# One list for projections, decode and attention, with pages two at a time

## The chip, the cores and the metric

The kernel runs on one core of a Trainium2 chip. The metric is device time in microseconds (us) of one execution; lower is better. Before the change the median of three runs is 1311.23 us (1310.11 to 1312.16).

## What is computed

One inference step of a two-layer trunk on 512 prompt tokens and on 8 x 4 sample tokens (32 rows), which are handled together as 544 columns. Layer 0 mixes tokens by a convolution module, layer 1 by stick-breaking attention with 16 heads of 64; each is followed by a ConvFFN (1024 to 2816 and back). The change touches layer 1's mixer alone, and the planner that orders several stages:

```python
qkv = (h @ attn_w_qkv[a]).reshape(b, t, 3, N_HEADS, HEAD_DIM)
q, k, v = qkv[:, :, 0], qkv[:, :, 1], qkv[:, :, 2]
k_all = jnp.concatenate([k_past[a], k], axis=1)
...
z = jnp.einsum('bqhd,bkhd->bhqk', q, k) * (HEAD_DIM ** -0.5) + bias
log_fail = jnp.where(valid, jax.nn.log_sigmoid(-z), 0.0)
after = lax.cumsum(log_fail, axis=3, reverse=True) - log_fail
weights = jnp.where(valid, jnp.exp(jax.nn.log_sigmoid(z) + after), 0.0)
out = jnp.einsum('bhqk,bkhd->bqhd', weights, v)
```

The prompt has no past. Each of the 8 sample sequences has 256 past positions, in two pages of 128 rows of a paged pool of keys and one of values. The new key and value rows are outputs too.

## The kernel before

Activations lie transposed: chunk c of 8 holds 128 channels (two heads) on the partitions and 544 tokens in the free dimension, in two streams, `SA` (256 columns) and `SB` (288, the sample tokens among them). Each projection is taken in three passes of rounded parts: weights and inputs are split into high and low (`whi`, `wlo`; `XH`, `XL`), and high x high, high x low and low x high are added. A chunk's weights are one slot (`W`, five slots at a time); ScalarE makes `whi` (L342), VectorE `wlo` (L345) from a 1 MB `raw` tile that SP's queue loads. A slot is 24 matmuls for `SA` and 24 for `SB`.

In program order around the change:

1. Queries of all chunks. `xT`, the residual, is stored to DRAM (`xsave`), and its place takes pages of the cache (`page_t`, three of them), decode weights (`wT`) and scratch.
2. The key stage, written out by hand. The keys of eight chunks are projected (`gemm`, L432 to L434); between the matmuls stand hooks. `page_turn` transposes a page of keys in eight 128x128 transposes (L1921), which VectorE and ScalarE copy out of PSUM half by half (L1922); `page_logits` multiplies it with `Qz`, eight products with 32 columns of weights each (L1934), of which four stand side by side in the array. An f32 product is two instructions. Rows of the new keys go back by transposes (L1883, and L1885 for the 32 sample rows).
3. The attention stage, a `Plan`: operations with an engine, an estimated cost and what they read and write; `Plan.run` (L162) emits them by simulated time, choosing for each engine the least of start time minus a share of the rank (the longest chain behind it), and its order is the engines' program order. PSUM tiles of one tag are handed out in the order of the list, and each waits for the users of the one before it in its bank. `values` projects value chunks (L2073 to L2075), `decode_weights` the sample tokens' weights, `page` multiplies one page of values with them (L2160, 32 columns of weights), `new_values` adds the new tokens' part (L2182), `pair` is a pair of heads on the prompt: in three units (`UNITS`) logits (L2214, 64 rows, two heads side by side in the array and in two banks of `z`), exponentials, suffix sums on VectorE, transposes (L2254, tag `t`), and products with the values (L2263, 64 columns of weights, two heads side by side, one trip for each unit). The pair's output goes through `qT` into `XH` and `XL` (L2292, L2293). Behind them `xT` returns from DRAM (L2288), and four chunks of the output projection begin in the attention stage's banks.
4. The rest of the output projection (L432 to L434 again), and from the adds of L2320 on the second ConvFFN.

The same `Plan.run` orders the convolution stage at the start and both ConvFFNs.

Of the kernel before, what the change touches and what calls it, by code (L numbers as in the profile page):

```python
# [73 lines left out]
STICK = 0.2  # L74
HI, LO = 0.59, 1.23

BIG = 1.0e17
E_BUFS, S_BUFS, W_BUFS = 3, 2, 3


class Plan:
# [15 lines left out]
    def op(self, eng, cost, fn, r=(), w=(), a=(), follows=None, lift=0.0, urgent=0.0, after=()):  # L97
# [33 lines left out]
        if follows is not None:  # L131
            self.follows[i] = follows
        return i
# [28 lines left out]
    def run(self):  # L162
# [16 lines left out]
        free, last = {}, {}  # L179
        while any(ready.values()):  # L180
            best = None
            for eng, q in ready.items():
                if q:
                    f = free.get(eng, 0.0)
                    i = min(q, key=lambda i: (max(f, start[i]) - self.eager * rank[i] - self.urgent.get(i, 0.0) -
                                              (STICK if self.follows.get(i, -1) == last.get(eng) else 0.0), i))
# [6 lines left out]
            fn()  # L193
            last[eng] = i
# [9 lines left out]
def tile_trunk(  # L204
# [78 lines left out]
    for c in range(0, 3 * NC, 2):  # L283
        both(attn_w_qkv[0], 0, NC, c)
    for c in range(0, NC, 2):
        both(attn_w_o[0], 0, NC, c)
# [1552 lines left out]
    pages = deque()  # L1839
    n_page = [0]  # L1840

    def gather():

        i = n_page[0]
        if i >= 4 * NB:
            return
        n_page[0] += 1
        t = page_t[i % PAGE_BUFS]
        j = i % (2 * NB)
        pool.indirect_dma_start(out=t, out_offset=None, in_=ck if i < 2 * NB else cv,  # L1850
                                in_offset=bass.IndirectOffsetOnAxis(ap=idx[:, j:j + 1], axis=0))
        pages.append(t)


    for _ in range(PAGE_BUFS):
        gather()

    q_all.stream(SB, hooked=False)
    d1_cm, d1 = open_pool("d1")
    Qz = d1.tile([P, NC, 2, 160], F32, name="Qz")  # L1860
    Qf = d1.tile([P, NC, 2, NS], F32, name="Qf")
    pool.memset(Qz, 0.0)
    pool.memset(Qf, 0.0)
    for bg in range(2):
        for j in range(2):
            rows = slice(j * HD, (j + 1) * HD)
            src = qT[rows, :, SEQ + 16 * bg:SEQ + 16 * bg + 16].rearrange("p c (b i) -> p c b i", b=4)
            dst = Qz[rows, :, bg, :].rearrange("p c (b s) -> p c b s", s=40)[:, :, :, 4 * j:4 * j + 4]
            pool.tensor_copy(dst, src)
            dst = Qf[rows, :, bg, :].rearrange("p c (b s) -> p c b s", s=8)[:, :, :, 4 * j:4 * j + 4]  # L1870
            pool.tensor_copy(dst, src)
# [3 lines left out]
    ps_cm, ps = open_pool("ps_qkv", space=PSUM)  # L1875
    banks.update(acc=3, tr=2, one=1)

    def rows_of(src, n, dst, dst_s):


        def turn(pt):
            for b in range(2):
                pe.transpose(pt[:, b * P:(b + 1) * P], src[:, b * P:(b + 1) * P], ident)  # L1883
            if n > 256:
                pe.transpose(pt[:NS, 256:256 + P], src[:, 256:n], ident)  # L1885

        def store(pt):
            dve.tensor_copy(dst, pt[:, :256].rearrange("p (b d) -> p b d", b=2))

        def store_s(pt):  # L1890
            if n > 256:
                act.copy(dst_s, pt[:NS, 256:256 + P])

        def steps():
            pt = bank("tr", uid("rows"))
            for f in (turn, store, store_s):
                f(pt)

        steps.parts = turn, store, store_s
        return steps  # L1900

# [4 lines left out]

# [458 lines left out]
```

## Time and profile before

| | us |
|---|---|
| median of 3 runs | 1311.23 (1310.11 to 1312.16) |
| span of the profiled execution | 1311.1 |
| TensorE busy (matmul / weight load) | 1292.6 / 1224.0 |
| VectorE, ScalarE, GpSimd busy | 985.8, 720.8, 158.8 |
| key stage, attention stage | 653 to 735, 735 to 884 |

The profile is that of one execution; its span is the time from the first to the last instruction. Busy times of TensorE overlap since matmuls are pipelined; where its time goes is better read from the starts of its instructions. "Idle before" names what ended an engine's wait.

### The profile page before, as it was taken

The numbers are of one execution on the slowest core, as the hardware profiler recorded it, in microseconds if no ns is written. First come the engines' busy times: TensorE is split into PE (matmuls) and PEld (weight loads), VectorE is DVE, ScalarE is ACT, GpSimd is POOL, SyncE is SP. The second block draws the span as 40 slices with busy tenths as digits, with TensorE's granted clock in tenths as the row PEclk, the third lists the DMA queues.
The fourth block names the chain that finished last, engine by engine and source line by source line (L and its number), as shares of the span: only waits on it lengthen the run. The fifth ranks groups of instructions, "written<-read, shape, count | busy, mean of one in ns | idle before, by whom it ended". The sixth has DMA issues, their size and how long they took to land. (4 is left out here: it accounts for less than half of the span.)

```text
span 1311.1 us, 27036 instructions
## 1 busy us (share of the span) xinstructions
PE 1292.6 (99%) x11072; PEld 1224.0 (93%) x11072; DVE 985.8 (75%) x1679; ACT 720.8 (55%) x1440; POOL 158.8 (12%) x302
## 2 busy tenths in 40 slices
PE   8999999999999999999999999999999999999997
PEld 7998689999999999999999877789999999999997
DVE  6799885978987877868234688775997996886864
ACT  6477584545554544445323688863655564454453
POOL 4000013101010010000222113210010010010000
PEclk9999999999999999999999999999999999999999
DMA  7463523123232233234456224432223332223221
GB/s 205 122 183 100 155 66 113 33 82 113 89 113 91 78 105 111 73 123 166 145 177 188 91 86 135 128 129 65 81 66 113 97 114 90 89 89 108 89 75 69
DMA packets 116592, 142.43 MB, mean 109 GB/s; under 512 B 5364, under 2 KB 107528, under 8 KB 116195
## 3 DMA queue, kind: packets, MB, share of 16 engines
q1 hardware_dynamic: 107151, 111.89, 27.5%
q0 software_dynamic: 9024, 28.78, 7.0%
q8 instruction: 87, 1.43, 0.5%
q14 instruction: 38, 0.31, 0.1%
q10 hardware_dynamic: 292, 0.02, 0.0%
HBM read 129.34 MB, written 12.18 MB: 108 GB/s over the span
## 5 line engine op out<-in xcount | busy, mean ns | idle before, releaser
L342 ACT CAST whi<-raw 128x1024 fp32r<-128x1024 f32 (+2 forms) x245 | 223.3, 913 | 149.3 <-PE tr L1317 31.6
L345 DVE TENSOR_TENSOR wlo<-raw,whi 128x1024 fp32r<-128x1024 f32 (+2 forms) x245 | 256.5, 1051 | 57.1 <-ACT whi L342 56.0
L673 PE MATMUL acc<-XH,whi 128*128 128x288 f32 (+1 forms) x384 | 114.3, 298 | 0.0
L674 PE MATMUL acc<-XL,whi 128*128 128x288 f32 (+1 forms) x384 | 111.6, 290 | 0.0
L675 PE MATMUL acc<-XH,wlo 128*128 128x288 f32 (+1 forms) x384 | 111.1, 289 | 0.2 <-DVE wlo L345 0.2
L432 PE MATMUL acc<-XH,whi 128*128 128x288 f32 (+1 forms) x360 | 107.8, 299 | 1.6 <-DVE xT L2320 1.1
L434 PE MATMUL acc<-XH,wlo 128*128 128x288 f32 (+1 forms) x360 | 103.8, 288 | 0.5 <-DVE wlo L345 0.5
L433 PE MATMUL acc<-XL,whi 128*128 128x288 f32 (+1 forms) x360 | 103.9, 289 | 0.0
L1552 ACT COPY G<-acc 128x272 f32<-128x272 f32 (+1 forms) x72 | 26.9, 374 | 104.9 <-PE acc L1518 90.1
L1516 PE MATMUL acc<-TH,whi 128*128 128x272 f32 x288 | 82.9, 288 | 0.0
L1518 PE MATMUL acc<-TH,wlo 128*128 128x272 f32 x288 | 82.8, 288 | 0.0
L1517 PE MATMUL acc<-TL,whi 128*128 128x272 f32 x288 | 82.8, 287 | 0.0
L673 PEld LDWEIGHTS acc<-XH,whi 128*128 128x128 f32 x384 | 72.9, 190 | 3.0 <-issue 1.6
L1317 PE MATMUL av<-HL,whi 128*128 128x288 f32 (+1 forms) x256 | 74.6, 291 | 0.3 <-DVE HL L1570 0.3
L1316 PE MATMUL av<-HH,whi 128*128 128x288 f32 (+1 forms) x256 | 74.4, 291 | 0.0
L1318 PE MATMUL av<-HH,wlo 128*128 128x288 f32 (+1 forms) x256 | 74.0, 289 | 0.3 <-DVE wlo L345 0.3
L1316 PE MATMUL tr<-HH,whi 128*128 128x256 f32 (+1 forms) x256 | 73.4, 287 | 0.0
L674 PEld LDWEIGHTS acc<-XL,whi 128*128 128x128 f32 x384 | 73.0, 190 | 0.3
L1317 PE MATMUL tr<-HL,whi 128*128 128x256 f32 (+1 forms) x256 | 73.3, 286 | 0.0
L675 PEld LDWEIGHTS acc<-XH,wlo 128*128 128x128 f32 x384 | 72.9, 190 | 0.4 <-DVE wlo L345 0.4
L1318 PE MATMUL tr<-HH,wlo 128*128 128x256 f32 (+1 forms) x256 | 72.9, 285 | 0.0
L432 PEld LDWEIGHTS acc<-XH,whi 128*128 128x128 f32 x360 | 67.7, 188 | 4.6 <-issue 2.4
(402 smaller groups left out, 4349.1 us busy)
## 6 DMA issues: line engine op xcount, KB each, us to landing
raw<-in_ffn_w_gate_dram SPq DMA_DIRECT2D x22, 1024.0 KB
raw<-in_ffn_w_up_dram SPq DMA_DIRECT2D x22, 1024.0 KB
raw<-in_ffn_w_down_dram SPq DMA_DIRECT2D x24, 768.0 KB
raw<-in_attn_w_qkv_dram SPq DMA_DIRECT2D x12, 1024.0 KB
raw<-in_conv_w_in_dram POOLq DMA_DIRECT2D x6, 1024.0 KB
rep<-glu SPq DMA_DIRECT2D x36, 142.0 KB
raw<-in_conv_w_out_dram POOLq DMA_DIRECT2D x4, 1024.0 KB
raw<-in_ffn_w_down_dram SPq DMA_DIRECT2D x8, 512.0 KB
```

The lines of the kernel that those rows point to most:

```text
L342: act.copy(hi[:, k, :], src[:, k])
L345: dve.tensor_tensor(lo[:, k, :], src[:, k], hi[:, k, :], op=ALU.subtract)
L432: pe.matmul(o, hi[:, k, :], xh[:, k, c0:c0 + n], start=(k == 0), stop=False)
L433: pe.matmul(o, hi[:, k, :], xl[:, k, c0:c0 + n], start=False, stop=False)
L434: pe.matmul(o, lo[:, k, :], xh[:, k, c0:c0 + n], start=False, stop=(k == nk - 1))
L673: pe.matmul(o, hi[:, k, :], XH[:, k, c0:c0 + n], start=(k == 0), stop=False)
L674: pe.matmul(o, hi[:, k, :], XL[:, k, c0:c0 + n], start=False, stop=False)
L675: pe.matmul(o, lo[:, k, :], XH[:, k, c0:c0 + n], start=False, stop=(k == NC - 1))
L1316: pe.matmul(o, hi[:, j + k, :], xh, start=(start and k == 0), stop=False, **kw)
L1317: pe.matmul(o, hi[:, j + k, :], xl, start=False, stop=False, **kw)
L1318: pe.matmul(o, lo[:, j + k, :], xh, start=False, stop=(stop and k == len(xs) - 1), **kw)
L1516: pe.matmul(o, hi[:, j + k, :], xh, start=(start and k == 0), stop=False, **kw)
```

## The change

The key stage's loop goes, and its work joins the attention stage's `Plan`. Keys and values are projected in turn (`TURNS`: two key chunks, then a value chunk and a key chunk alternately), with their weights loaded in that order, and these projections are marked as `fill`. `page_logits` takes both pages of a sequence in one trip of 256 columns, with turned pages in the place of the last four chunks of `kT`; `sequence` multiplies both value pages in one trip; a pair's products go in one trip, save the last pair's. Sample columns of keys and values stay apart (`kT_s`, `vT_s`) and are turned all at once (`new_rows`); their weights form a block-diagonal matrix (`Zw`). The attention output's splits of the first seven pairs stand behind the last value projection, the last pair's are made from PSUM. PSUM's eight banks are dealt out anew. `Plan.run` gets a new key: work that starts within `NEAR` of the soonest goes ahead, in this list `fill` goes last, a change of shape (`form`) has a cost and waits up to `PATIENT`.

```diff
--- before.py
+++ after.py
...
+CHANGE, CHANGE_BIAS = 0.17, 3.0
...
-E_BUFS, S_BUFS, W_BUFS = 3, 2, 3
+E_BUFS, S_BUFS, W_BUFS = (3, 1), (1, 1), (3, 1)
+NEAR, PATIENT = 0.15, 2.0
...
-        free, last = {}, {}
+        free, last, form = {}, {}, None
...
+        def turned(i):
+            return self.change if self.change and self.ops[i][0] == "pe" and self.forms.get(i) != form else 0.0
...
-                    i = min(q, key=lambda i: (max(f, start[i]) - self.eager * rank[i] - self.urgent.get(i, 0.0) -
-                                              (STICK if self.follows.get(i, -1) == last.get(eng) else 0.0), i))
+                    soon = min(max(f, start[i]) for i in q) + NEAR
+
+                    def key(i):
+                        t, turn = max(f, start[i]), turned(i)
+                        later = t > soon or i in self.fill or (turn and self.fill and form is None and start[i] + PATIENT > soon)
+                        return (bool(later), t + CHANGE_BIAS * turn - self.eager * rank[i] - self.urgent.get(i, 0.0) -
+                                (STICK if self.follows.get(i, -1) == last.get(eng) else 0.0), i)
...
+            cost += turned(i)
+            if eng == "pe":
+                form = self.forms.get(i)
...
-    for c in range(0, 3 * NC, 2):
+    for c in range(0, NC, 2):
         both(attn_w_qkv[0], 0, NC, c)
+    TURNS = [("k", 0), ("k", 1)] + [x for c in range(NC) for x in (("v", c), ("k", c + 2)) if x[1] < NC]
...
+    specs.extend((r0 + c // 2 * 2 + (f == "v"), c % 2, c % 2 == 1, NC) for f, c in TURNS)
...
-    banks.update(acc=1, one=1, av=1, z=3, t=2)
+    banks.update(acc=2, one=1, dz=1, av=1, z=2, t=1)
...
-    def values(i, h):
...
+    def project(slot, h):
+
...
+        pt = psum("acc")
...
+            last = plan.op("pe", 6 * n * COL, weighted(pt, slot, h, q), w=[pt], follows=last, after=[] if last is None else [last],
+                           r=[("slot", slot), ("X", 2 * q), ("X", 2 * q + 1)])
+            plan.fill.add(last)
...
+        if h:
+            prepare(slot + SPLIT_BUFS)
+        return pt
...
+    def keys(c, h):
+        c0, n = (SA, SB)[h]
+        pt = project(k0 + TURNS.index(("k", c)), h)
+        plan.op("act", acost(256), lambda: act.copy(kT[:, c, c0:c0 + 256], pt()[:, :256]),
+                r=[pt], w=[("k", c, h)] + ([("ktp", i) for i in range(4)] if c >= 4 else []))
...
+            plan.op("act", 0.2, lambda: act.copy(kT_s[:, c, :], pt()[:, 256:n]), r=[pt], w=[("kT_s", c)])
+        rows, src = to_rows(lambda b: kT[:, c, c0 + b * P:c0 + (b + 1) * P], [("k", c, h)])
...
+    def values(c, h):
+        n = (SA, SB)[h][1]
+        pt = project(k0 + TURNS.index(("v", c)), h)
+        vt = plan.tile("vT", 2, lambda: vts_.tile([P, SA[1]], F32, tag="vT", name=uid("vT"), bufs=2))
+        plan.op("act", acost(256), lambda: act.copy(vt(), pt()[:, :256]), r=[pt], w=[vt])
...
+    def new_rows(cols, r, dst):
...
+        def turn():
+            for g in range(2):
+                pe.transpose(rows()[:, g * P:(g + 1) * P], cols(g), ident)
+
+        def store():
+            for j in range(4):
+                nc.sync.dma_start(out=dst[:, :].rearrange("t (g j d) -> t g j d", g=2, j=4)[:, :, j, :], in_=new_s[32 * j:32 * j + 32])
+
+        plan.op("pe", 0.22, turn, r=r, w=[rows])
+        plan.op("act", 0.35, lambda: act.copy(new_s, rows()[:, :2 * P].rearrange("p (g d) -> p g d", g=2)),
+                r=[rows], w=["new", "Qz"])
+        plan.op("sp", 3.0, store, r=["new"])
...
+    def page_logits(n):
...
+        for pg in range(2):
+            t = page(2 * n + pg)
+            for half in range(2):
+                pt = psum("t")
...
+                plan.op("pe", 0.43, turn, r=[t, (t, 1), "pages"], w=[pt])
...
+                    r=[pt], w=[("ktp", 2 * pg + half)])
...
+        def logits():
             for g in range(2):
                 for s in range(4):
                     c = 4 * g + s
...
+                    pe.matmul(z()[32 * s:32 * s + 32, g * KW:(g + 1) * KW], Qz[:, c, 32 * b:32 * b + 32], kt[:, c, :],
+                              start=(b == 0 and g == 0), stop=(b == 3), skip_group_check=True)
...
+        plan.op("pe", 0.86, logits, r=[("ktp", i) for i in range(4)] + ["Qz"], w=[z], form="c32")
...
+    def sequence(n):
...
+        ts = [page(2 * NB + 2 * n + pg) for pg in range(2)]
+        pt = psum("dz")
...
+        def f():
+            for g in range(2):
+                for pg in range(2):
+                    for s in range(4):
+                        c = 4 * g + s
+                        pe.matmul(pt()[32 * s:32 * s + 32, g * P:(g + 1) * P], wT[:, 2 * bg + g, pg, 32 * s:32 * s + 32],
+                                  ts[pg]()[:, c * P:(c + 1) * P], start=(g == pg == 0), stop=(pg == 1), skip_group_check=True)
+
+        plan.op("pe", 0.9, f, r=[*ts, *((t, 1) for t in ts), ("wT", 2 * bg), ("wT", 2 * bg + 1), "pages"], w=[pt], form="c32")
...
-                for i in range(4):
-                    c = 4 * g + i
-                    pe.matmul(pt()[32 * i:32 * i + 32, g * P:(g + 1) * P], wn[:, 2 * bg + g, 32 * i:32 * i + 32],
-                              vtok_s[:, c * P:(c + 1) * P], start=(g == 0), stop=True, skip_group_check=True)
+                pe.matmul(pt()[:, g * P:(g + 1) * P], wn[:, 2 * bg + g, :], new_s[:, g, :],
...
-        plan.op("pe", 1.0, new, r=[("vnew", i) for i in range(NC)] + [("wn", 2 * bg), ("wn", 2 * bg + 1)], w=[pt])
-        plan.op("dve", 0.37, lambda: dve.tensor_tensor(o, pt()[:, :2 * P], o, op=ALU.add), r=[pt], w=[("oacc", bg)])
+        plan.op("pe", 0.45, new, r=["new", "pages", ("wn", 2 * bg)], w=[pt])
...
             z = [psum("z") for _ in range(2)]
-            e, s, w = sbuf("e", 1024, E_BUFS), sbuf("s", 1024, S_BUFS), sbuf("w", 1024, W_BUFS)
+            e, s, w = (sbuf(f"{tag}{n}", 2 * n, bufs[n < 512]) for tag, bufs in (("e", E_BUFS), ("s", S_BUFS), ("w", W_BUFS)))
...
-            plan.op("pe", 2.2e-3 * n + 0.1, logits, r=[("q", c)], w=z)
+            plan.op("pe", 1.69e-3 * n, logits, r=[("q", c), ("k", c, 0), ("k", c, 1)], w=z, form="r64")
...
+        def products(us, cost, key):
+            def f():
+                for u in us:
...
+            plan.op("pe", cost, f, form="c64", w=[key],
+                    r=[*((ws[u], j) for u in us for j in range(2)), ("vtok", c % 3, 0), ("vtok", c % 3, 1)])
+
+        def out(lo, n, src, r, key):
+            cols = slice(lo, lo + n)
+            plan.op("act", acost(n), lambda: act.copy(XH[:, c, cols], src(cols)), r=r, w=[("XH", c, key)], a=[("X", c)])
+            plan.op("dve", dcost(n), lambda: dve.tensor_tensor(XL[:, c, cols], src(cols), XH[:, c, cols], op=ALU.subtract),
+                    r=[*r, ("XH", c, key)], a=[("X", c)])
+
+        if c < NC - 1:
+            products(range(len(UNITS)), 2.1, av)
...
+            held_out.append(lambda: out(0, SEQ, lambda cols: qT[:, c, cols], [("q", c)], 0))
+        else:
+            for u in range(len(UNITS)):
+                products([u], 0.82e-3 * 2 * sum((i + 1) * P for i, _ in UNITS[u]), (av, u))
+            for u in range(len(UNITS)):
+                for i, _ in UNITS[u]:
+                    out(i * P, P, lambda cols: av()[:, cols], [(av, u)], i)
...
+    both_halves(keys, 0)
+    both_halves(keys, 1)
...
     for c in range(NC):
+        if c < 2:
+            for n in range(4 * c, 4 * c + 4):
+                page_logits(n)
+        if c == 2:
+            decode_weights()
+        if c + 2 < NC:
+            both_halves(keys, c + 2)
+        if c == 5:
+            new_rows(lambda g: kT_s[:, 4 * g:4 * g + 4, :].rearrange("p c t -> p (c t)"), [("kT_s", i) for i in range(NC)], ksv)
+            new_logits()
...
-            chunk(c + 1)
-        for p in (2 * c, 2 * c + 1):
-            page(p)
-        if c == NC - 1:
+            both_halves(values, c + 1)
...
+        if c == 7:
+            new_rows(lambda g: vT_s[:, 4 * g:4 * g + 4, :].rearrange("p c t -> p (c t)"), [("vT_s", i) for i in range(NC)], vsv)
+        for n in {3: (0,), 4: (1, 2), 5: (3, 4), 6: (5, 6), 7: (7,)}.get(c, ()):
+            sequence(n)
...
+        if c == 7:
+            while held_out:
+                held_out.pop(0)()
         pair(c)
     plan.op("sp", 3.0, lambda: nc.sync.dma_start(out=xflat, in_=xsave), w=["pages"] + [("wT", t) for t in range(4)])
-    plan.op("sp", 3.0, lambda: nc.sync.dma_start(out=vsv, in_=vtok_s[:NS, :]), r=[("vnew", i) for i in range(NC)])
...
-    for i, tag in enumerate(("acc", "z", "z", "z")):
+    for i, tag in enumerate(("acc", "z", "z", "one")):
...
```

## Rows read from the trace of the kernel before

**Rows 1.** The page's first section: busy us of each engine, share of the span, instructions.
```profile
PE 1292.6 (99%) x11072; PEld 1224.0 (93%) x11072; DVE 985.8 (75%) x1679; ACT 720.8 (55%) x1440; POOL 158.8 (12%) x302
```

**Rows 2.** Busy time by stretch: from and to, length, then PE, PEld, DVE, ACT, POOL busy us (with instructions), granted clock, DMA share, GB/s. The first ConvFFN, the key stage, the attention stage.
```profile
215.00:598.00 383.00, 382.06 (x3038) 380.08 (x3037) 301.01 (x490) 192.97 (x343) 32.38 (x85) 1.00 0.30 95
...
653.00:735.00 82.00, 82.00 (x859) 76.22 (x863) 31.53 (x50) 27.48 (x51) 18.86 (x25) 1.00 0.56 176
735.00:884.20 149.20, 145.39 (x1438) 115.78 (x1424) 118.44 (x186) 116.64 (x213) 33.83 (x48) 1.00 0.34 108
```

**Rows 3.** TensorE's groups by line and shape, 653 to 886: line, operation, out<-in, rows*columns of the array, shape, count | busy us, mean ns | idle before.
```profile
L2263 PE MATMUL av<-w,vtok 128*64 128x128 f32 x320 | 22.3, 280 | 0.0
...
L1934 PE MATMUL dz<-ktp,Qz 128*32 128x128 f32 x256 | 10.3, 279 | 0.0
L2160 PE MATMUL one<-xT 128*32 128x128 f32 x256 | 10.3, 279 | 0.8 <-DVE vtok L2106 0.8
...
L2103 PE MATMUL one<-ident,vT 128*32 128x128 f32 x8 | 2.2, 272 | 0.0
L1885 PE MATMUL rows<-ident,kT 128*32 128x128 f32 x8 | 2.2, 272 | 0.0
...
L2133 PE MATMUL one<-ident,Zn 128*32 128x128 f32 x4 | 1.1, 272 | 0.0
```

**Rows 4.** TensorE in order of time, around a page's logits in the key stage: start us, length us, line, operation, count.
```profile
655.99 0.28 PE L434 MATMUL acc<-XH,wlo 128*128 128x256 f32 x1
656.20 0.65 PE L1934 MATMUL dz<-ktp,Qz 128*32 128x128 f32 x16
656.77 0.39 PE L432 MATMUL acc<-XH,whi 128*128 128x256 f32 x1
657.00 0.28 PE L433 MATMUL acc<-XL,whi 128*128 128x256 f32 x1
657.11 0.28 PE L434 MATMUL acc<-XH,wlo 128*128 128x256 f32 x1
```

**Rows 5.** The same view, products between two value pages, and the projection behind them.
```profile
867.43 1.09 PE L2263 MATMUL av<-w,vtok 128*64 128x128 f32 x16
868.46 0.64 PE L2160 MATMUL one<-xT 128*32 128x128 f32 x16
869.03 0.39 PE L2073 MATMUL z<-XH,whi 128*128 128x256 f32 x1
```

**Rows 6.** The same view, logits of 512 columns and what comes next: the first and the last of the five slow groups (the others are of smaller shapes), and one of the quick ones.
```profile
735.16 1.87 PE L2214 MATMUL z<-kT,qT 64*128 64x512 f32 x4
736.96 0.40 PE L2073 MATMUL acc<-XH,whi 128*128 128x288 f32 x1
...
761.85 1.13 PE L2214 MATMUL z<-kT,qT 64*128 64x512 f32 x4
763.65 0.41 PE L2254 MATMUL t<-ident,e 128*128 128x128 f32 x2 [0.68 <-DVE e L2247]
...
849.52 1.13 PE L2214 MATMUL z<-kT,qT 64*128 64x512 f32 x4
850.58 0.33 PE L2254 MATMUL t<-ident,e 128*128 128x128 f32 x1
```

**Rows 7.** The same view, the first key projection and the first matmul behind the attention stage.
```profile
653.00 0.38 PE L432 MATMUL acc<-XH,whi 128*128 128x256 f32 x1 [0.50 <-ACT qT L1771]
...
884.17 0.37 PE L432 MATMUL acc<-XH,whi 128*128 128x288 f32 x1 [1.13 <-DVE xT L2320]
```

**Rows 8.** All engines in order of time: a page's transposes and the copy of its first half.
```profile
653.83 1.03 PE L1921 MATMUL kt<-ident,xT 128*128 128x128 f32 x8
...
654.46 0.69 DVE L1922 COPY ktp<-kt 128x512 f32<-128x512 f32 x1 [9.27 <-PE kt L1921]
```

**Rows 9.** The same view: the issue of `xT`'s return, and the first add on it.
```profile
869.16 0.34 SPq L2288 DMA_DIRECT2D xT<-xsave  x1
...
882.37 0.42 DVE L2320 TENSOR_TENSOR xT<-acc,xT 128x256 f32<-128x256 f32 x1 [3.53 <-PE acc L2075]
```

**Rows 10.** Stretches of 2 us behind that issue, columns as in rows 2; the last figure is GB/s.
```profile
874.00:876.00 2.00, 2.00 (x28) 1.47 (x26) 0.02 (x1) 0.74 (x2) 0.00 (x0) 1.00 0.97 418
876.00:878.00 2.00, 2.00 (x28) 1.78 (x28) 0.52 (x1) 1.21 (x2) 0.00 (x0) 1.00 0.07 26
```

**Rows 11.** TensorE in order of time at the kernel's start.
```profile
27.28 0.38 PE L916 MATMUL tr<-ident,xr 128*128 128x128 f32 x2
29.80 0.57 PE L953 MATMUL tr<-dg,mean_m 128*128 128x128 f32 x1 [2.14 <-DVE XL L925]
```

**Rows 12.** The stretch behind it, columns as in rows 2; the granted clock is the last figure but two.
```profile
29.80:36.70 6.90, 6.90 (x27) 5.82 (x28) 4.56 (x10) 3.42 (x9) 0.00 (x0) 0.51 0.01 4
```

**Rows 13.** The page's fifth section, the costliest group of ScalarE.
```profile
L342 ACT CAST whi<-raw 128x1024 fp32r<-128x1024 f32 (+2 forms) x245 | 223.3, 913 | 149.3 <-PE tr L1317 31.6
```

More of the change, by code (lines that the diff above doesn't have):

```diff
@@ L95, in __init__, with op @@
         self.lift, self.urgent = {}, {}
-    def op(self, eng, cost, fn, r=(), w=(), a=(), follows=None, lift=0.0, urgent=0.0, after=()):
+        self.forms, self.change = {}, 0.0
+        self.fill = set()
+    def op(self, eng, cost, fn, r=(), w=(), a=(), follows=None, lift=0.0, urgent=0.0, after=(), form=None):
         i = len(self.ops)
@@ L132, in op @@
             self.follows[i] = follows
+        if form is not None:
+            self.forms[i] = form
         return i
@@ L1869, in tile_trunk @@
-            pool.tensor_copy(dst, src)
-            dst = Qf[rows, :, bg, :].rearrange("p c (b s) -> p c b s", s=8)[:, :, :, 4 * j:4 * j + 4]
-            pool.tensor_copy(dst, src)
+            rows, src = rows_q(j, bg)
+            pool.tensor_copy(Qf[rows, :, bg, :].rearrange("p c (b s) -> p c b s", s=8)[:, :, :, 4 * j:4 * j + 4], src)
     act_table("natural_log_exp_and_others")
     close(ps_cm)
[L1875 to L1900, printed above, removed]
@@ L2140, in tile_trunk @@
-    held = list(pages)
-    def page(p):
-        bg, b, pg = p // 8, p // 2 % 4, p % 2
-        t = plan.tile("page", PAGE_BUFS, lambda: page_t[(2 * NB + p) % PAGE_BUFS])
-        if p >= len(held):
-            def gather_():
-                pool.indirect_dma_start(out=t(), out_offset=None, in_=cv,
-                                        in_offset=bass.IndirectOffsetOnAxis(ap=idx[:, p:p + 1], axis=0))
-            plan.op("pool", 1.25, gather_, w=[t, ("asked", p)])
-            plan.op(f"page{p}", 4.0, lambda: None, r=[("asked", p)], w=[(t, 1)])
-        pt = psum("one")
-        def f():
+                pe.transpose(rows()[:, b * P:(b + 1) * P], src(b), ident)
@@ L2174, in new_values @@
     def new_values(bg):
-        pt, t = psum("one"), psum("one")
+        pt, t = psum("dz"), psum("one")
         o = oacc[:, bg, :]
@@ L2257, in unit @@
                 plan.op("act", acost(n), lambda j=j, t=t: act.copy(two(w)[:, j, :n], t()[:, :n]), r=[t], w=[(w, j)])
-            def products():
-                for i, lo in parts:
-                    for kc in range(i + 1):
-                        for j in range(2):
-                            pe.matmul(av()[HALF[j], i * P:(i + 1) * P], vtok[c % 3][:, kc, HALF[j]],
-                                      two(w)[:, j, lo + kc * P:lo + (kc + 1) * P],
-                                      start=(kc == 0), stop=(kc == i), skip_group_check=True)
```

324 lines of the change are left out of this document (141 added, 183 removed).

## Prediction, made before the change was run

> **What bounds the kernel now.** The page's first section was read first: TensorE is busy for 1292.6 us of a 1311.1 us span, VectorE for 985.8 and ScalarE for 720.8 [rows 1]. A busy share says little on pipelined matmuls, so the stages came next, in stretches of time. In the first ConvFFN the granted clock is 1.00 and TensorE is without a gap [rows 2]; such a stage becomes shorter only by fewer matmuls. The change lies in 653 to 884, where keys (82 us) and then the rest of attention (149.2 us) run one after the other [rows 2]. In the key stage VectorE works 31.53 us of 82 and ScalarE 27.48; in the attention stage both work nearly 80% of the time, TensorE has gaps, and its sums of busy time hide more. So the starts of its instructions were read, group by group. Three things cost time there that is not arithmetic: turns from one shape of matmul to another [rows 4, 5], logits whose two heads don't run side by side [rows 6], and a wait at either end [rows 7].
>
> **What a turn costs.** Within the projections one 256-column matmul starts 0.11 us after the other (657.00 to 657.11) [rows 4]. Before a page's logits the gap is 0.21 (655.99 to 656.20): 0.10 for going in. The first projection after it takes 0.23 (656.77 to 657.00): 0.12 for coming back. Going out is found by two runs of 16 instructions: value pages run four side by side, so 4 waves, in 0.57 us (868.46 to 869.03), products two side by side, so 8 waves, in 1.03 us (867.43 to 868.46) [rows 5]. That is (1.03 - 0.57) / 4 = 0.115 a wave, and 0.57 - 4 x 0.115 = 0.11 is left for going out. A trip alone costs 0.10 + 0.11 + 0.12 = 0.33 us. Where trips follow on each other, as products and pages do [rows 5], going in and coming back are paid once, and 0.11 is the least.
>
> **The parts.**
>
> *Fewer trips.* Pages go two at a time: `page_logits` makes 8 trips of twice the columns, where 256 instructions in 16s made 16 [rows 3], and `sequence` makes 8 of twice the instructions instead of 16. A pair's products go in one trip for seven pairs and three for the last: 10 in place of 24. The two of `new_values` become full-shape matmuls: 2 less. That is 8 + 8 + 14 + 2 = 32 trips. Their waves stay: twice the columns cost twice a wave, at most. Bounds: 32 x 0.11 = 3.5 and 32 x 0.33 = 10.6 us. The key stage's 8 stood alone (0.33, 2.6 us); for the other 24 I take 0.25, nearer to the upper end since a projection follows on most: 6.0. **Minus 8.6 us.**
>
> *New rows in one piece.* The 16 small transposes of 32 columns (L1885 and L2103) and 4 of `Zn` (L2133) go [rows 3]; 4 for key and value rows and 4 for `Zw` come. One of 128 columns is taken at a wave's 0.115: 12 x 0.115 = **minus 1.4 us**. ScalarE gains 16 copies of 32 columns where it had as many of rows: nothing, under TensorE.
>
> *Keys as a filler.* Five logits groups between 735.16 and 761.85 are slow; the first takes 1.80 us and the last 1.80 (the next work starts at 736.96 and 763.65), where the same shape takes 1.06 later (849.52 to 850.58) [rows 6]. Over the quick time of their own shapes the five lose some 4 us: the second head waits for a bank of `z`, or VectorE isn't done. With keys and values to fill in, the attention stage's load spreads: VectorE's 31.53 + 118.44 and ScalarE's 27.48 + 116.64 [rows 2] over some 219 us are 68% and 66%. But `z` goes from three banks to two, so the wait can return anywhere. Bounds: minus 4, and plus 14 if the 19 quick groups lose 0.74 each. I take **minus 3**, near the first, since the list now holds a logits group back until it has been ready for 2 us, by when the other head's bank is mostly free.
>
> *One bank for transposes.* `t` goes from two banks to one. Four transposes of a page start at 653.83, the copy starts at 654.46 and takes 0.69 [rows 8]: the bank is held 1.3 us. There are 32 such turns of pages and 48 of pairs: 80 x 1.3 = 104 us of some 219. The first 38 (all pages and pair 0) follow on each other in list order, 49 us; projections cover the gaps: one weight slot is 48 matmuls, 48 x 0.12 = 5.8 us, and 16 slots are 92 us. If that cover is gone, each turn costs its copy, about 0.8 us. The Trainium skill's Perfetto Trace Analysis, Optimizing Tensor Performance, has independent groups rotate through different banks, so that a copy overlaps the next matmuls; by that rule this edit costs time, and the sum would be the third rival's 1312. No row of before shows a single bank; the rows give only how long it is held.
>
> *New chains.* The fifth chunk's key copy must wait for all page logits, whose turned pages lie in its place in `kT`; seven slots of projections (41 us) and the pages' own work stand ahead of it, against 49 us of turns: about even. `xT`'s return from DRAM must now wait for the value projections' end, a transpose, a copy, four stores of `new_s` on SP's queue and two matmuls, where it waited for pages alone. It was issued at 869.16 [rows 9], its traffic ends soon after 876 [rows 10], and the first add that needs it stands at 882.37 [rows 9]: 6 us of cover. Four output groups (4 x 24 x 0.12 = 11.5 us) still come behind the last value projection, against an estimated 5 us of chain and 7 of transfer. What is late next is L2320's adds, and behind them everything. Bounds 0 and 6 (both waits, 3 each); I take **plus 1**.
>
> *At no cost.* The output's splits for seven chunks move behind the last value projection: on ScalarE and VectorE, covered by the four output groups; without that cover the last pair would show about 1.5 us. SP has some 14 more issues and long idle; POOL's gathers and selects stay as many. The waits at 653.00 (0.50) and 884.17 (1.13) [rows 7] stay: all banks change hands at both in either version.
>
> *The other lists.* `Plan.run` also orders the convolution stage and both ConvFFNs. The new key puts whatever starts within 0.15 us ahead of more important work that is not ready. In the ConvFFNs TensorE has no gap to lose [rows 2]. At the start there is one: 2.14 us idle until 29.80 [rows 11], and from there to 36.70 the granted clock is 0.51, the lower level of 1.2 GHz [rows 12], which costs half of 6.9. I take 0; bounds minus 5.5 (2.1 + 3.4, both go) and plus 5.5 (as much again).
>
> **The sum.** -8.6 - 1.4 - 3 + 1 + 0 = -12.0. The profiled execution's span is 1311.1, 0.1 under the median of 1311.23 and inside the runs' 1310.11 to 1312.16, so **1299 us**.
>
> **The rivals.**
> - *More than that (1293).* The start's idle goes too, and the lower clock with it: 1299 - 5.5. For it: the new rule fills gaps. Against it: the start is ordered by arrivals.
> - *Less (1305).* Trips merged already, so 0.11 each (3.5 in place of 8.6), or half of the slow logits come back. For it: [rows 5]; against it: the key stage's lone trips [rows 4].
> - *One bank holds TensorE up (1312, no change).* Projections fail as cover in the page stretch, and half of the 32 page turns show their 0.8 us: 16 x 0.8 = 13 lost against 12 gained. It decides against a measurable gain from 12 turns on (9.6 us). Against it: the projections are ready at any time.
> - *The new rule hurts the ConvFFNs (slower, 1317).* A cast (913 ns in the mean [rows 13]) goes ahead of a bank's copy because it is ready first; TensorE waits for the bank. By `PASSES` the two ConvFFNs make 36 gate and up quads of two chunks; 0.5 us in each is 18 lost, so 1299 + 18. It decides from 12 / 36 = 0.33 us in each. For it: the zero gaps rest on the old order. Against it: VectorE is idle for a fifth of that stage [rows 2], room to catch up.
>
> - *The list doesn't interleave (1302).* Projections first, then attention, as now: only the first two parts and the new chains remain, 1311.1 - 8.6 - 1.4 + 1. It lies inside the forecast's own range and has its chance in there.
>
> **How the numbers follow.** Under 0.2% (2.6 us) a measurement can't tell this kernel from no change. The forecast's own range, 1295 to 1303, has 0.45; more than that 0.13; less, 1303 to 1308.6, 0.23; no change (the bank, around 1312) 0.08; slower (the ConvFFNs, or the bank with more turns) 0.11. Faster is 0.45 + 0.13 + 0.23 = 0.81. The range is 1290 to 1311: under it 0.05, above it 0.13.
>
> **What would show it.** In the changed profile: 16-instruction runs of page logits are 8, each near 1.0 us; products in one run of about 2.3 us per pair; logits groups near 1.06 also early; no idle of TensorE behind the turned pages' copies; `xT`'s return landing before L2320's counterpart; the ConvFFNs as long as they were. The prediction is wrong if TensorE waits for `t`, for `z`, for weights or for `xT`, or if a stage outside 653 to 884 changes by over 3 us.

## The result, and the profile after

The changed kernel takes 1293.8 us in the median, the one before 1311.7 beside it; the ratio is 0.9856 (95% interval 0.9841 to 0.9872), 17 to 21 us faster. One of the four runs of the changed kernel took 3321.5 us and is left out of the ratio; the median of the other three is 1293.6, the number that the expectations below start from. The forecast was 1299 in a range of 1290 to 1311: the direction and the range held, but the time lies below the forecast's own range of 1295 to 1303, and 6 of the 18 us were not foreseen. Most of those 6 lie outside the list that the change rewrites.

The profile after, first the page's first section (busy us, share of the span, instructions; before in [rows 1]), then busy time by stretch (columns as in [rows 2]): to the first ConvFFN, from there to the queries, the queries, the list of keys, values, decode and pairs, what is left of the output projection, the second ConvFFN with the end.

```profile
PE 1274.7 (99%) x10908; PEld 1220.0 (94%) x10908; DVE 981.1 (76%) x1671; ACT 718.5 (56%) x1448; POOL 158.5 (12%) x301
```

```profile
0.00:221.46 221.46, 217.02 (x2111) 193.51 (x2111) 181.37 (x343) 147.82 (x414) 39.45 (x64) 1.00 0.48 138
221.46:598.32 376.86, 374.76 (x2979) 373.51 (x2980) 302.00 (x497) 191.62 (x342) 29.36 (x78) 1.00 0.29 92
598.32:648.16 49.84, 49.12 (x389) 48.75 (x387) 25.20 (x64) 20.17 (x36) 5.32 (x8) 1.00 0.55 183
648.16:864.98 216.82, 214.96 (x2110) 187.43 (x2109) 147.32 (x228) 145.81 (x274) 52.72 (x71) 1.00 0.46 141
864.98:902.45 37.47, 37.47 (x292) 37.29 (x291) 22.43 (x43) 15.56 (x27) 0.00 (x0) 1.00 0.28 85
```

The first matmul of the first ConvFFN, before and after:

```profile
225.42 0.38 PE L1316 MATMUL av<-XH,whi 128*128 128x256 f32 x1
```

```profile
221.46 0.38 PE L1343 MATMUL av<-XH,whi 128*128 128x256 f32 x1
```

It stood at 225.42 and stands at 221.46; the first key projection at 653.00 [rows 7] and 648.16; the first matmul behind the list at 884.17 [rows 7] and 864.98. So the span's 19.1 us are 4.0 ahead of the first ConvFFN, 0.9 between there and the keys, and 14.35 in the list (231.17 to 216.82); from its end to the kernel's end nothing changed (426.9 and 427.0). VectorE and ScalarE now work 68% and 67% of the list's time, close to the 68% and 66% of the prediction.

**The list.** TensorE in order of time, around two pages' logits, where one page stood alone in [rows 4], and a pair's products, in pieces in [rows 5]:

```profile
656.18 0.60 PE L2078 MATMUL t<-ident,xT 128*128 128x128 f32 x4
656.71 1.07 PE L2090 MATMUL dz<-kT,xT 128*32 128x256 f32 x16
657.71 1.13 PE L2210 MATMUL z<-kT,qT 64*128 64x512 f32 x4
658.77 0.66 PE L2078 MATMUL t<-ident,xT 128*128 128x128 f32 x4
...
840.34 2.40 PE L2266 MATMUL av<-w,vtok 128*64 128x128 f32 x40
842.67 0.44 PE L2000 MATMUL one<-ident,vT 128*128 128x128 f32 x2
```

A run of two pages takes 1.00 us, a pair's products 2.33, and the logits behind the pages follow in the next shape with no projection between. These logits, the first of the list, take 1.06 (657.71 to 658.77): the 1.80 of [rows 6] is gone. No wait for `t` stands in the pages' stretch.

To compare lists, each was taken apart in the same way. Every matmul in a run of one shape is put at the interval at which such matmuls start (0.118 us for 256 columns of a projection, 0.133 for 288, 0.109 for 128 columns of the others, divided by how many stand side by side). The transposes of 32 columns before the change count as full-shape work at 0.109, since they start at that distance and show no turn. What a run takes beyond that is its turn, the cost of the change from one shape to another; where it is over 0.35, all but 0.17 is booked as a wait. What a stretch at the lower clock adds is booked in the same way, for the most part with the waits.

```
                  list us   turns   plain work   time of turns (each)   waits
before             231.2     144      199.6        24.6  (0.171)          6.9
after              216.8      85      198.2        14.7  (0.173)          3.8
```

The price of a turn comes out the same in both, and in every variant below (0.166 to 0.175). So the list's 14.35 are 9.9 for 59 turns, 1.4 of plain work (the small transposes), and 3.1 of waits. The Trainium skill's TensorEngine Tiling (Array Packing), Key Properties, says that changing the tiling mode drains TensorE, without a figure; these traces agree in that a change costs time, 0.17 us each, and do not show by themselves that it is a drain.

**The start.** TensorE at the place of [rows 11] and [rows 12], with the stretch's busy times behind it:

```profile
30.64 0.40 PE L700 MATMUL acc<-XH,whi 128*128 128x288 f32 x1
...
32.35 0.94 PE L980 MATMUL tr<-dg,mean_m 128*128 128x128 f32 x6
33.22 0.40 PE L700 MATMUL acc<-XH,whi 128*128 128x288 f32 x1
```

```profile
27.00:36.70 9.70, 9.70 (x73) 9.12 (x73) 7.06 (x14) 6.68 (x15) 0.00 (x0) 1.00 0.48 123
```

The six matmuls for the mean waited 2.14 us and then ran with the granted clock at 0.51, the 1.2 GHz level, until 36.70. Now they come later in the order and find all they need, with projections ahead of them, and the granted clock in this stretch is 1.00, the 2.4 GHz level.

### The profile page after: what moved, and what is told of

Read it like the earlier page. It is cut to its first block, busy times and chain, and to the rows that moved or that the text cites. A ratio compares the mean times of both kernels' runs of the same rounds, so it can differ in the third digit from the quotient of the medians.

```text
span 1292.0 us, 26645 instructions
## 1 busy us (share of the span) xinstructions
PE 1274.7 (99%) x10908; PEld 1220.0 (94%) x10908; DVE 981.1 (76%) x1671; ACT 718.5 (56%) x1448; POOL 158.5 (12%) x301
## 4 chain that ended last, share of the span: by engine, by line
PE 92%; DVE 3%; issue 2%; ACT 1%; DMA 1%; DVEq 0%; POOL 0%; ACTq 0%; POOLq 0%; SPq 0%
PE acc L1545 5%; PE acc L1543 5%; PE acc L1544 5%; PE acc L700 4%; PE acc L701 4%; PE acc L702 4%; PE av L1343 3%; PE acc L460 3%; PE acc L459 3%; PE acc L461 3%; PE av L1344 3%; PE av L1345 3%; PE tr L1343 3%; PE tr L1344 3%; PE tr L1345 3%; PE tr L1545 3%
## 5 line engine op out<-in xcount | busy, mean ns | idle before, releaser
L700 PE MATMUL acc<-XH,whi 128*128 128x288 f32 (+1 forms) x384 | 114.4, 298 | 0.0
L701 PE MATMUL acc<-XL,whi 128*128 128x288 f32 (+1 forms) x384 | 110.8, 288 | 0.0
L702 PE MATMUL acc<-XH,wlo 128*128 128x288 f32 (+1 forms) x384 | 110.3, 287 | 0.0
L1970 PE MATMUL acc<-XH,whi 128*128 128x256 f32 (+1 forms) x264 | 82.8, 314 | 0.6 <-ACT XH L2275 0.6
L1971 PE MATMUL acc<-XL,whi 128*128 128x256 f32 (+1 forms) x264 | 76.2, 289 | 0.1
L1972 PE MATMUL acc<-XH,wlo 128*128 128x256 f32 (+1 forms) x264 | 75.9, 287 | 0.0
L700 PEld LDWEIGHTS acc<-XH,whi 128*128 128x128 f32 x384 | 72.3, 188 | 2.8 <-issue 1.6
L1484 DVE SCALAR_TENSOR_TENSOR cv<-G,fprm,cv 128x560 f32<-128x560 f32 x88 | 69.4, 796 | 0.5
```

Source lines behind the costliest of these rows:

```text
L700: pe.matmul(o, hi[:, k, :], XH[:, k, c0:c0 + n], start=(k == 0), stop=False)
L701: pe.matmul(o, hi[:, k, :], XL[:, k, c0:c0 + n], start=False, stop=False)
L702: pe.matmul(o, lo[:, k, :], XH[:, k, c0:c0 + n], start=False, stop=(k == NC - 1))
L1970: pe.matmul(o, hi[:, k, :], XH[:, k, c0:c0 + n], start=(k == 0), stop=False)
```

## The experiments

**Whose is the start?** Two runs cross the order rule with the rest of the change: the changed kernel with the old rule outside the attention list,

```diff
 t, turn = max(f, start[i]), turned(i)
+if not self.change:
+    return (False, t - self.eager * rank[i] - self.urgent.get(i, 0.0) -
+            (STICK if self.follows.get(i, -1) == last.get(eng) else 0.0), i)
```

and the kernel before with the new rule in all its lists.

```diff
-i = min(q, key=lambda i: (max(f, start[i]) - self.eager * rank[i] - ...
+soon = min(max(f, start[i]) for i in q) + 0.15
+i = min(q, key=lambda i: (bool(max(f, start[i]) > soon), max(f, start[i]) - self.eager * rank[i] - ...
```

> The changed kernel, with the new order rule kept for the attention list alone; the convolution stage and both ConvFFNs are put in order by the old rule. Theory (the rule is worth some 4 us at the start, nothing in the ConvFFNs, and the rest of the gain is in the attention list): the first matmul of the first ConvFFN comes at 225.4 again and not at 221.5, with 2.1 us of idle near 29.8 and the lower clock behind it; the attention list lasts 216.8 as in the changed kernel; the time is 1293.6 + 4 = 1297.6 us. Rival 1 (the early start was chance, a clock that happened to rise at another moment): 1293.6. Rival 2 (the rule also helps the ConvFFNs' order): over 1299.

> The kernel before, with the new order rule (what starts within 0.15 us goes first) in all its lists and nothing else of the change. Theory (the start alone): first ConvFFN at 221.5, attention stage 149.2 with its five slow logits, 1311.5 - 4 = 1307.5 us. Rival 1 (the rule alone also removes the slow logits, which then have nothing to do with the keys as a filler): 1303.5. Rival 2 (the early start is chance): 1311.5.

Measured: 1298.38 us (ratio 0.9902, 0.9887 to 0.9918) and 1307.2 us (0.9968, 0.9958 to 0.9978). The first has its ConvFFN at 224.6 and a list of 216.9, the second 221.2 and 231.3. Both say the same: the rule is worth 4.6 us (1298.4 against 1293.8; 5.7 against the 1292.7 of the repeat below) or 4.8 (1312.0, the kernel before beside it, against 1307.2), ahead of the keys, and nothing in the list. In the first, TensorE's idle is back, and behind it the granted clock is 0.50 from 32.26 to 35.67:

```profile
30.34 0.93 PE L983 MATMUL tr<-dg,mean_m 128*128 128x128 f32 x5 [2.81 <-DVE XL L955]
```

The second says one thing more. With the new rule the logits of the old list take 2.5 us less (23.7 us in all for 26.2), and the list is as long as before: TensorE now waits for the single bank of projections, and at the end.

```profile
PE acc L433 <- DVE xT L2321: 1.8, 1, 1.8
PE acc L2074 <- ACT vT L2097: 1.7, 3, 0.8
```

So quicker logits alone were worth nothing in this list. It is not a full cure: three of its groups still take 1.31 to 1.80 us.

**Trips.** Four runs undo the merging: the products of a pair in three operations; one page to an operation, key pages and value pages both; the list's price of a turn at 0; and all three.

```diff
-products(range(len(UNITS)), 2.1, av)
+for u in range(len(UNITS)):
+    products([u], 0.82e-3 * 2 * sum((i + 1) * P for i, _ in UNITS[u]), (av, u))
...
```
```diff
...
-plan.op("pe", 0.86, logits, r=[("ktp", i) for i in range(4)] + ["Qz"], w=[z], form="c32")
+plan.op("pe", 0.43, logits, r=[("ktp", 2 * pg), ("ktp", 2 * pg + 1), "Qz"], w=[z], form="c32")
...
-plan.op("pe", 0.9, f, r=[*ts, *((t, 1) for t in ts), ("wT", 2 * bg), ("wT", 2 * bg + 1), "pages"], w=[pt], form="c32")
+plan.op("pe", 0.45, f, r=[ts[pg], (ts[pg], 1), ("wT", 2 * bg), ("wT", 2 * bg + 1), "pages"], w=[pt], form="c32")
```
```diff
-plan.change = CHANGE
+plan.change = 0.0
```

> The changed kernel with the products of a pair in three trips again instead of one, for all eight pairs: 14 more trips. Theory (a trip is 0.25 us here): +3.5, 1297.1 us, with 24 runs of products of 1.02, 1.02 and 0.59 us. Bounds of a trip: 14 x 0.11 = 1.5 (1295.1) and 14 x 0.33 = 4.6 (1298.2). Rival (the gain of the list came from projections as a filler, trips are nothing): 1293.6.

> The changed kernel with one page to a trip, in the key pages' logits and in the value pages' products: 16 more trips with the same waves. Theory: key pages stood alone (8 x 0.33 = 2.6), value pages 8 x 0.25 = 2.0, together +4.6, 1298.2 us, with 32 runs of 16 instructions at 0.57 us. Bounds: 16 x 0.11 = 1.8 (1295.4) and 16 x 0.33 = 5.3 (1298.9). Rival (pages fall next to each other or to other narrow work in the list anyway, so that a merged trip saves nothing): 1293.6.

> The changed kernel, whose attention list no longer prices a turn from one shape of matmul to another (the price is 0, so logits aren't held back for 2 us either); the merged trips stay. The list then comes out with 46 runs of full-shape work for 37, and 50 narrow runs for 49. Theory A (turns cost, the slow logits are gone for the spread of the load): 9 times 0.22 for going in and coming back = +2.0, 1295.6 us, logits still 1.06. Theory B (the holding back is what removed the slow logits): also 5 slow logits, 1295.6 + 4 = 1299.6. Rival (the list's price of a turn does nothing, the merged operations do it all): 1293.6.

> As the one before, without a price of a turn, and with the products of a pair in three trips and one page to a trip as well: all merging is undone, by hand and by the list. The list comes out with 59 full-shape runs for 37, 30 runs of pages and new keys' logits for 17, 19 runs of products for 8. Theory (trips are the larger part of the gain): 24 x 0.11 + 22 x 0.22 = +7.5, 1301.1 us. Rival 1 (trips are nearly free, since splitting the products alone cost nothing): 1295. Rival 2 (slow logits come back on top): 1305.

Measured, with the lists taken apart as above:

```
                      us       ratio (interval)           list us  turns   time of turns   waits
products by unit    1292.8    0.9863 (0.9848 to 0.9878)    217.0     92       15.7          2.8
one page            1295.24   0.9875 (0.9857 to 0.9892)    219.5    103       17.5          3.6
no price of a turn  1292.3    0.9868 (0.9851 to 0.9884)    216.7     95       15.8          2.5
all three           1300.3    0.9925 (0.9908 to 0.9941)    225.3    131       22.1          4.9
```

One by one they cost 0.1, 2.7 and nothing; together 8.4 of 216.8. Merging by hand and the list's own price stand in for each other: with the products split, the list still put the three parts of five pairs out of eight together, and 14 more operations became 7 more turns; with the price at 0, the merged operations keep most trips whole. Only with both gone do 46 turns come back, and they cost what turns cost (7.4 us, and 1.1 of waits). The slow logits don't return, but for one of 1.37 us in the list with one page to an operation; there is none without a price of a turn, so holding logits back for 2 us is not what keeps them away.

In three of the lists TensorE also waits for a value page's gather, 0.8 us with one page to an operation and more in two others. The waits of the list without a price, and of the one with all three undone:

```profile
PE dz L2152 <- DMA xT<-in_cache_v_dram,idx: 1.4, 1, 1.4
```

```profile
PE dz L2153 <- DMA xT<-in_cache_v_dram,idx: 3.2, 1, 3.2
```

Behind the second of these the granted clock is 0.50 from 804.37 to 807.79. The wait of 3.2 us and an estimated half of those 3.4 us make the 4.9 us of waits of that list.

**The filler and the banks.** One run takes the projections' low priority away, the other gives the second projection bank to the transposes.

```diff
-plan.fill.add(last)
```
```diff
-banks.update(acc=2, one=1, dz=1, av=1, z=2, t=1)
+banks.update(acc=1, one=1, dz=1, av=1, z=2, t=2)
```

> The changed kernel, whose projections are no longer the lowest in priority (and logits aren't held back): the list ranks them like the rest, with the price of a turn kept. It comes out with 28 full-shape runs for 37. Theory (projections as a filler cover the waits of the single bank for transposes and of the two for logits): 9 x 0.22 = 2.0 less for turns, but slow logits (+4) and waits for the transposes' copies (some 6) when projections are used up: 1301 us. Rival (the spread of keys and values over the stage does it without a priority): 1291.6.

> The changed kernel with two banks for transposes and one for projections, where it has one and two. Theory (one bank for transposes costs nothing, projections cover its copies, while one bank for projections makes each of 32 wait about 0.3 us for its copy unless other work stands between): 1296 us, TensorE waiting at `acc`. Rival (the single bank holds transposes up, hidden in the list's order): 1290.

Measured: 1296.16 us (0.9901, 0.9884 to 0.9917) and 1300.87 us (0.9936, 0.992 to 0.9953). Without the priority the list has 9 turns fewer (13.0 us for 14.7) but 7.7 us of waits for 3.8: 219.2 us, a third of the loss that was expected. Two banks for transposes made it worse by 8.2, to 225.1 us, three times the loss that was expected: 11.8 us of waits. The largest part that the profile names, 4.6 us in nine waits, is where a transpose of new rows waits for ScalarE's copy out of the one projection bank.

```profile
PE one L2000 <- ACT vT L2022: 2.7, 5, 1.0
PE one L2000 <- ACT kT L2008: 1.9, 4, 0.5
```

Of the two, the scarce bank is the projections', not the transposes'.

**Keys and values in turn.** All keys first, then all values, with the page logits between the fourth and the fifth key chunk; the rest of the change stays.

```diff
-TURNS = [("k", 0), ("k", 1)] + [x for c in range(NC) for x in (("v", c), ("k", c + 2)) if x[1] < NC]
+TURNS = [(f, c) for f in "kv" for c in range(NC)]
...
-both_halves(keys, 0)
-both_halves(keys, 1)
+for c in range(4):
+    both_halves(keys, c)
+for n in range(8):
+    page_logits(n)
+for c in range(4, NC):
+    both_halves(keys, c)
...
-    if c + 2 < NC:
-        both_halves(keys, c + 2)
```

> The changed kernel with keys and values no longer projected in turn: all eight key chunks first, then the eight value chunks; one list, merged trips and the price of a turn stay (its order has 84 runs for 86, so turns cost the same). Theory (the spread of the pairs' work over both projections is what removed the waits at the logits): the pairs' work crowds behind the last key projection, waits of 3 to 8 us come back at `z`, `t` or for VectorE, 1297 to 1301 us. Rival (the low priority of projections alone is enough): 1293.6.

Measured: 1307.69 us (0.9968, 0.9955 to 0.9981), far beyond either expectation. The list has 83 turns (14.4 us) and takes 230.9 us, as long as before the change: 18.1 us of waits eat the whole gain. TensorE in order of time, where the pages end:

```profile
705.89 1.07 PE L2090 MATMUL dz<-kT,xT 128*32 128x256 f32 x16
708.45 0.66 PE L2078 MATMUL t<-ident,xT 128*128 128x128 f32 x4 [1.50 <-DVE kT L2082]
709.84 0.66 PE L2078 MATMUL t<-ident,xT 128*128 128x128 f32 x4 [0.73 <-ACT kT L2082]
711.28 0.71 PE L2078 MATMUL t<-ident,xT 128*128 128x128 f32 x4 [0.79 <-DVE kT L2082]
712.72 1.12 PE L2250 MATMUL t<-ident,e 128*128 128x128 f32 x4 [0.73 <-ACT kT L2082]
```

```profile
711.76:718.59 6.83, 6.10 (x36) 4.27 (x35) 1.73 (x4) 3.57 (x7) 0.94 (x1) 0.50 0.53 178
```

Two things that the prediction priced as dangers are seen here. By the order of the edit, the fifth chunk's key copy has to wait for the last page logits; no projection starts between 705.08 and 716.82, and the single bank `t` stands bare: the four waits are for copies out of it, 1.50 us once and 0.73 to 0.79 three times. Behind these waits the granted clock falls to 0.50, the 1.2 GHz level, from 711.76 to 718.59. And at the end `xT`'s return is late: SP issues it at 868.68, the first add needs it at 876.83, and TensorE waits for that add (the next three lines are of SP's queue, VectorE and TensorE).

```profile
868.68 0.34 SPq L2322 DMA_DIRECT2D xT<-xsave  x1
```

```profile
876.83 0.42 DVE L2349 TENSOR_TENSOR xT<-acc,xT 128x256 f32<-128x256 f32 x1 [4.57 <-DMA xT<-xsave]
```

```profile
877.40 0.37 PE L459 MATMUL acc<-XH,whi 128*128 128x288 f32 x1 [3.30 <-DVE xT L2349]
```

In the changed kernel the return is issued at 852.17, and the first add comes at 863.05 and waits for TensorE's sum, not for it:

```profile
852.17 0.34 SPq L2323 DMA_DIRECT2D xT<-xsave  x1
```

```profile
863.05 0.42 DVE L2350 TENSOR_TENSOR xT<-acc,xT 128x256 f32<-128x256 f32 x1 [0.59 <-PE acc L1972]
```

Of the 18.1 us of waits the profile names 4.1 for copies of turned pages and 3.3 for `xT`'s add; the lower clock is at most an estimated 3.4, half of its 6.8 us. The rest are smaller waits; logits are slow in it only once.

**What is left to gain.** The list of the changed kernel still waits 0.69 and 0.61 us at the last pair. TensorE there:

```profile
857.51 1.97 PE L2266 MATMUL av<-w,vtok 128*64 128x128 f32 x32
860.17 0.66 PE L2266 MATMUL av<-w,vtok 128*64 128x128 f32 x8 [0.69 <-DVE XL L2276]
860.76 0.39 PE L1970 MATMUL acc<-XH,whi 128*128 128x256 f32 x1
...
861.98 0.38 PE L1970 MATMUL acc<-XH,whi 128*128 128x256 f32 x1 [0.61 <-ACT XH L2275]
```

Three more runs: a page's landing planned 7 us behind its gather in the list without a price; the last pair's products counted as full-shape work, in the changed kernel; and the changed kernel once more.

```diff
-plan.change = CHANGE
+plan.change = 0.0
...
-plan.op(f"page{i}", 4.0, lambda: None, r=[("asked", i)], w=[(t, 1)])
+plan.op(f"page{i}", 7.0, lambda: None, r=[("asked", i)], w=[(t, 1)])
```
```diff
-plan.op("pe", cost, f, form="c64", w=[key],
+plan.op("pe", cost, f, form="c64" if c < NC - 1 else None, w=[key],
```

> The changed kernel without a price of a turn (as in the run e5), and with the landing of a page planned as 7 us behind its gather instead of 4, since TensorE waited 1.4 us for one value page there. 97 runs. Theory: that wait goes, and the attention list lasts 216.7 - 1.4 = 215.3 us, 1292 us as a whole. Rival (the gather is late because its buffer comes free late): 216.7.

> The changed kernel with the products of the last pair counted as full-shape work, so that the list sees no turn in them; nothing else. In the changed kernel these 40 products come in one run of 3.25 us with 0.69 of waiting in it, and the first projection behind waits 0.61 for the output's split. Theory (the price of the turn holds the two first parts back until the third is ready): two runs, both waits gone, the list lasts 216.8 - 1.3 + 0.3 = 215.8 us, 1292.6 as a whole. Rival (the last part itself is late, its waits remain): 216.8.

> The changed kernel once more, beside the others. The clock behind the warm-up rose at 5.1 us in some runs of the new order and at 10 in others (among them the profiled run of the changed kernel), with 1.7 us between the two at the first convolution matmul. If that is chance, this run comes out at either, with the first ConvFFN at 219.5 to 221.5 and all stages behind it as they were, 1292 to 1294.5 us; if it belongs to the kernel's order, at 221.5 again.

Measured: 1292.77 us (0.985, 0.9837 to 0.9863), 1290.44 us (0.9835, 0.9822 to 0.9848) and 1292.68 us (0.9852, 0.9839 to 0.9865). The page's wait is gone, but the list is 216.05 us and not 215.3: 0.6 of its 1.4 us were won, and why not the rest stays open. The last pair's products now come apart, 32 and then 8, earlier, with work behind them that covers the splits:

```profile
849.83 1.97 PE L2266 MATMUL av<-w,vtok 128*64 128x128 f32 x32
851.73 0.44 PE L2177 MATMUL one<-ident,oacc 128*128 128x128 f32 x2
852.33 0.66 PE L2266 MATMUL av<-w,vtok 128*64 128x128 f32 x8 [0.16 <-ACT XH L2275]
```

That list takes 215.27 us where the repeat of the changed kernel takes 216.84, and its times (1289.98 to 1290.99) lie below all of the repeat's (1291.63 to 1293.50); the two intervals of the ratio still overlap a little. It is the fastest version measured.

## Why the prediction was right, and where it fell short

**Fewer trips, -8.6.** Right in size, not in its account. The runs of pages, new keys' logits and products fell by the 32 that were counted, from 57 to 25. In the list 59 turns went with them, at 0.17, which is 9.9 us; counted by the 32 trips that is 0.31 each, close to the 0.33 of a lone trip, where 0.25 was taken. But the prediction gave each merged operation its own share, 14 x 0.25 = 3.5 for the products, and undoing those alone cost 0.1. The list that orders the trips has a price of a turn too, and the sum left that edit out as if it did nothing. The unit to count is the turn in the list as it comes out, not the edit.

**New rows, -1.4.** Plain work fell from 199.6 to 198.2. That is 12 transposes fewer at their measured distance of 0.109 us, a count as in the prediction; no run undoes this edit by itself.

**Slow logits, -3, and new chains, +1.** Together -2, measured -3.1 of waits. The logits are quick (from 26.2 us to 22.2 in all) and no wait shows on the new chains. The wait of 1.13 us at the list's end [rows 7], which the prediction let stay, is gone too; against it stand 1.3 us of new waits at the last pair, which it took as covered. Its reason, that the list holds logits back, is refuted by the run without a price of a turn. What removed them is not settled. The five are not of one kind: in the first of [rows 6] the four matmuls start 0.53, 0.22 and 0.53 us apart, one after the other, while in the last they start in pairs 0.01 apart, like the quick ones, and the time goes in the wait of 0.68 for VectorE. They stay away in most variants; one group is slow again with one page to an operation (1.37 us), without the filler (1.64), with one bank for projections (2.12) and with keys first (1.78).

**One bank for transposes.** The rival at 1312 did not come: with projections ready as cover, as the prediction argued, TensorE waits 0.2 us for `t` in the whole list. Its price was right, 0.73 to 0.79 us in three of four turns once that cover is gone, as the run with keys first shows. The rule of the Trainium skill's Perfetto Trace Analysis, Optimizing Tensor Performance, on rotating banks, which would have made this edit dear, does not hold for `t` here, where projections fill the time of the copy; it does for `acc`: giving the projections' second bank to `t` cost 8.2 us. The prediction gave that second bank no line at all.

**The list doesn't interleave (1302).** Mis-sized. No run takes the interleaving away as a whole; the nearest is the one where keys go first, at 1307.7. The rival counted only a gain not made, and not that the single bank, the place of the turned pages and the late return of `xT` then lie bare. Projecting keys and values in turn is what covers these edits.

**The other lists, 0.** This is the step that failed: "I take 0", since "the start is ordered by arrivals". The profile after shows 4.0 us there, and the crossed runs 4.6 and 4.8 in the time. That is over the 3 us for a stage outside 653 to 884 by which the prediction would call itself wrong; the time is still inside the forecast range because that was drawn wide, down to 1290. Its own bound, minus 5.5 for the idle and the lower clock, was near the measured number, and the rival *more than that* (1293) named the mechanism; it had 0.13. What spoke against it was an argument without a row: the 2.14 us in [rows 11] end with VectorE's `XL`, a matter of order, not with a DMA, and the DMA share behind them is 0.01 [rows 12]. The ConvFFNs were not hurt by the rule: from the first one's first matmul to the keys the time is 0.9 us less, and the second one's stretch is as it was.

## What to carry to other kernels

Count the changes of matmul shape in the order as it comes out, multiply by one measured price, and leave single edits without a price until both means that merge trips are known. A bank count is read together with what fills TensorE while the bank is held: the same single bank was free here beside projections and cost its whole copy without them. And an edit in a shared planner is a change to every list that it orders; where one of them shows an idle that ends with another engine's ordinary work, such an edit can win it.

## What was not expected of the hardware

The rise of TensorE's clock at the kernel's start moves from execution to execution of one and the same kernel, and a view of the granted clock can hide it. In the profiled run of the changed kernel five transposes start 0.21 us apart, ahead of 10.18; in the repeat of the same kernel, 0.11 (the first two lines, then the others, TensorE in order of time).

```profile
8.59 1.27 PE L943 MATMUL tr<-ident,xr 128*128 128x128 f32 x5
...
10.18 2.24 PE L994 MATMUL warm<-zero 128*128 128x256 bf16 x19
```

```profile
6.81 0.71 PE L943 MATMUL tr<-ident,xr 128*128 128x128 f32 x5
...
7.69 2.24 PE L994 MATMUL warm<-zero 128*128 128x256 bf16 x19
```

```profile
5.40:10.18 4.78, 4.78 (x27) 4.57 (x27) 2.51 (x6) 1.46 (x5) 2.43 (x6) 1.00 1.15 281
```

The last line is the slow stretch of the first of the two, with a granted clock of 1.00. That figure is not a measurement: the trace's record of the granted clock begins at 10.05 us in this execution and at 4.44 in the repeat, with 1.00 in both, and the view counts a stretch ahead of the first record as 1.00. The matmuls agree with the record. In all 14 profiled executions those of the warm-up start 0.21 us apart ahead of it and 0.11 behind it. It begins at 9.9 to 10.6 us in three (the changed kernel's own, the kernel before with the new rule, one page to a trip) and at 4.3 to 6.0 in the others, the kernel before among them. The first ConvFFN starts at 221.46 after the late rise and in the repeat here:

```profile
219.46 0.38 PE L1343 MATMUL av<-XH,whi 128*128 128x256 f32 x1
```

So the 4.0 us that the profile shows at the start are 6.0 where both executions have the early rise. The Trainium skill's TensorE: Matmul & The Clock Gate, The HAM clock gate, says that the moment varies from run to run; these rows agree. It also says that the gate's records were seen to be unreliable; no run here shows that.
